# Tail products of a two-layer encoder taken 512 columns wide with tokens as rows, and two more weight groups split by adding transfers

## The chip, the cores and the metric

The kernel runs on one core of one Trainium2 chip. The metric is device time in microseconds (us) of one execution, as the median of several runs. The kernel before takes 1712.34 us (three runs, 1711.75 to 1714.05).

The core's engines are named as the profile names them: PE is the matrix engine (PEld are its weight loads), DVE the vector engine, ACT the scalar engine, POOL the general-purpose engine, SP the engine that only issues transfers here. Each engine takes its instructions in the order in which they are written. A matmul multiplies a stationary operand (loaded by PEld, 128 x 128 here) with a moving operand that streams past it, and adds into a PSUM bank of 128 partitions x 512 float32.

## The reference

256 tokens of width 1024 pass two layers. Each layer normalises, projects to 18688 columns, runs three token mixers, and merges them by token-wise gates:

```python
for l in range(DEPTH):
    h = rmsnorm(x, norm_g[l])
    proj = h @ w_in[l]                     # 1024 x 18688
    (a_q, a_ff, a_fb, a_i, a_g, b_q, b_k, b_v, b_g, c_s, c_g, merge) = split(proj)
    y_a = hgrn2_mixer(a_q, a_ff, a_fb, a_i, ...) * silu(a_g)      # 256 x 1024
    y_b = retention_mixer(b_q, b_k, b_v, ...) * silu(b_g)         # 256 x 2048
    y_c = rwkv7_mixer(c_s, ...) * silu(c_g)                       # 256 x 1024
    gates = sigmoid(merge.reshape(b, t, 3, 1024))
    mixed = (gates[:, :, 0] * (y_a @ w_branch_a[l])
             + gates[:, :, 1] * (y_b @ w_branch_b[l])
             + gates[:, :, 2] * (y_c @ w_branch_c[l]))
    x = x + mixed @ w_out[l]
return rmsnorm(x, final_norm_g)
```

## The kernel before

**Precision.** Every product with a weight matrix is made of three float32r matmuls: a value v is split into hi (v rounded to float32r) and lo (v - hi), and a*b is taken as hi*hi + lo*hi + hi*lo. Float32r runs the PE faster than plain float32; the mixers' own small products are plain float32, and each of those stands as two matmul records in the trace.

**Weights.** Weights are laid out ahead of time in blocks of 1024 x 256, each as two halves of 128 partitions x 1024 numbers (512 KB). A half passes through rings of buffers: `in` (3), `hi` (5), `lo` (4). There are two ways to split it. The usual one: SP transfers the raw half into an `in` buffer, ACT copies it with rounding into `hi` (a CAST), DVE subtracts `hi` from the raw half into `lo`. The other one, for the block names in `CCE` (mixer A's five groups): POOL issues a transfer into `hi` that rounds, ACT writes its negative into `lo`, and POOL issues a second transfer of the same half that adds onto `lo`. This needs no `in` buffer and no DVE work, but two POOL-issued transfers.

**A layer** has two parts. In the first, mixer C runs in eight steps (head pairs p): `c_prep` and `c_solve` run two steps ahead of `c_scan`; between them stand the four `a_pair` steps (p = -1 to 2), then the four `b_pair` steps (p = 3 to 6). A `b_pair` projects query and key (blocks `bq`, `bk`), and for each of two heads value and gate (`bv`, `bg`): six blocks, twelve halves. `c_solve` needs a small POOL MEMSET of the diagonal of `c_M` before its DVE chain, and `c_prep` one of `c_ux`. In the second part, `tail`, the mixers' outputs (reloaded and split by `load_y`) are merged. For mixer m and column block b of 256 (four of them), the tail makes the gate's projection (`mg`), its sigmoid on ACT and DVE, the branch product (one weight block, two for B), multiplies by the gate and adds to the accumulator. Before the change the stationary operand in these is the weight (128 output features) and the moving one the activations of all 256 tokens (`feat_mm`): outputs have features as partitions, so the accumulators can be the stationary operand of the last product (`tok_mm`, `wo`), whose output has tokens as partitions. Every float32r matmul of the kernel streams 256 columns.

**Order.** Nothing is issued as written. All operations are recorded (`note`), with what each waits for (`parts` finds overlaps by pieces of 16 columns x 32 partitions); `cost` estimates each, and `order` places them by a list schedule, whose result is each engine's fixed program order. So all instructions carry the line of the one loop that issues them: L453 before, L460 after. `cost` and `order` hold the planner's figures for transfers and matmuls; a change in them moves instructions on every engine.

**Names in the trace.** `pj` and `c` (two PSUM banks each) hold the weight products, `n`, `s`, `ab` the mixers' small ones. `w_in`, `w_hi`, `w_lo` are the weight rings. In the tail, which reuses the mixers' buffers under names ending in `_t`, `ab_ex_t`/`ab_e_t` are mixer A's split output, `c_Z_t` B's, `c_rkvg_t`/`c_tu_t` C's, `ab_vg_t` the gates, `ab_kq_t`/`ab_c_t` the accumulators, `c_wa_t`/`c_qm_t` the split merged value (`m_hi`, `m_lo`), `c_bd_t` the residual x.

Of the kernel before, what the change touches and what calls it, by code (L numbers as in the profile page):

```python
# [19 lines left out]
D = 1024  # L20
# [4 lines left out]
TOK = ("ai", "bv", "wo")  # L25
# [3 lines left out]
CCE = ('aff', 'afb', 'aq', 'ai', 'ag')  # L29
# [34 lines left out]
def _blocks():  # L64
# [8 lines left out]
    for p in range(4):  # L73
        r.append((("bq", p), "w_in", 0, [(5120 + 256 * p, 256)]))
        r.append((("bk", p), "w_in", 0, [(6144 + 256 * p, 256)]))
        for h in (2 * p, 2 * p + 1):
            r.append((("bv", h), "w_in", 0, [(7168 + 256 * h, 256)]))
            r.append((("bg", h), "w_in", 0, [(9216 + 256 * h, 256)]))
    for m in range(3):
        for b in range(4):  # L80
            c = 256 * b
            r.append((("mg", m, b), "w_in", 0, [(15616 + 1024 * m + c, 256)]))
            for n, w, r0 in ((("wa", "w_branch_a", 0),), (("wb0", "w_branch_b", 0), ("wb1", "w_branch_b", 1024)),
                             (("wc", "w_branch_c", 0),))[m]:
                r.append(((n, b), w, r0, [(c, 256)]))
    for b in range(4):
        r.append((("wo", b), "w_out", 0, [(256 * b, 256)]))
# [3 lines left out]
for _i, _b in enumerate(_blocks()):  # L91
    BK[_b[0]] = _i
assert len(BK) == NBLK
# [28 lines left out]
class Plan:  # L122
# [3 lines left out]
    def __init__(self, ctx, tc, some):  # L126
# [4 lines left out]
        self.homes, self.base, self.top, self.place, self.turn, self.psum, self.ndram, self.cache = {}, {}, 0, {}, {}, {}, 0, {}  # L131
        self.last, self.readers, self.bank, self.fill = {}, {}, {}, {}
        self.width, self.tenant, self.before = dict(HOMES), {}, {}
        self.width.update({f"w_{k}{i}": 1024 for k, m in RW.items() for i in range(m)})
        for n, k in BANKS:
            for i in range(k):
                t = self.pp.tile([128, 512], F32, name=f"{n}{i}")[:, :]
                self.psum[n, i] = t
                self.base[t.tensor.name] = (None, f"{n}{i}")
# [3 lines left out]
    def home(self, n, era, dt):  # L143
        old = self.tenant.get(n)
        if old is None or self.tiles[old][1] != era:
            k, w = len(self.tiles), self.width[n]
            if old is not None:
                top, size = self.tiles[old][3], 4 * (w // 16 + 2)
                self.before[k] = {p for g in range(top, top + size) for p in [self.last.get(g, -1)] + self.readers.get(g, [])} - {-1}
            self.tiles.append((n, era, dt, self.top, bass.AP(tensor=self.some.tensor, offset=k << 20, ap=[[w, 128], [1, w]]), w))  # L150
            self.top += 4 * (w // 16 + 2)
# [3 lines left out]
    def real(self, ap):  # L155
# [3 lines left out]
        if k not in self.made:  # L159
            n, era, dt, _, _, w = self.tiles[k]  # L160
# [47 lines left out]
    def dram(self):  # L208
        plan = self

        class Dram:
            def tile(self, shape, dt, name, tag=None):
                plan.ndram += 1
                t = plan.dp.tile(shape, dt, name=f"{name}_{plan.ndram}")[:]
                plan.base[t.tensor.name] = (plan.top, 0)
                plan.top += int(np.prod(shape)) // 32 + 1
# [10 lines left out]
    def parts(self, ap):  # L227

        off = int(ap.offset)
        if ap.tensor.name == self.some.tensor.name:  # L230
            if off < 1 << 20:
                return ()
            _, _, _, base, _, w = self.tiles[off >> 20]
            off &= (1 << 20) - 1
        else:
            b = self.base.get(ap.tensor.name)
            if b is None:
                return ()
            base, w = b
            if base is None:  # L240
                return w
        dims = tuple((int(s), int(c)) for s, c in ap.ap)
        key = (base, off, dims)
        r = self.cache.get(key)
        if r is None:
            if w:
                p, c = divmod(off, w)
                ix = np.array([c])
                for s, n in dims[1:]:
                    if s:  # L250
                        ix = (ix[:, None] + s * np.arange(n)).ravel()
                ix = np.unique(ix // 16)
                r = [base + 4 * int(i) + q for q in range(p // 32, (p + dims[0][1] - 1) // 32 + 1) for i in ix]
            else:
                ix = np.array([off])
                for s, n in dims:
                    if s:
                        ix = np.unique((ix[:, None] + s * np.arange(n)).ravel())
                r = [base + int(i) for i in np.unique(ix // 32)]
            self.cache[key] = r  # L260
        return r
# [12 lines left out]
    def note(self, eng, op, args, kw):  # L274
# [4 lines left out]
        pred, true, rd, wr, fresh = set(), set(), [], [], False  # L279
        for a, w in aps:  # L280
            p = self.parts(a)
            if isinstance(p, str):
                if p in self.bank:
                    pred.add(self.bank[p])
                self.bank[p] = n
            else:
                (wr if w else rd).extend(p)
                if w and (op == "copy_predicated" or "accum_op" in kw):
                    rd.extend(p)
        last, readers = self.last, self.readers  # L290
        for g in rd:
            if g in last:
                true.add(last[g])
        for g in wr:
            if g in last:
                pred.add(last[g])
                pred.update(readers.get(g, ()))
            else:
                fresh = True
        if fresh and out.tensor.name == self.some.tensor.name:  # L300
            pred |= self.before.get(int(out.offset) >> 20, set())
        for g in rd:
            readers.setdefault(g, []).append(n)
        for g in wr:
            last[g] = n
            readers[g] = []
# [6 lines left out]
    def cost(self, eng, op, out, ins, args, kw):  # L313
# [3 lines left out]
        def psum(a):  # L317
            return self.base.get(a.tensor.name, (0,))[0] is None

        both = False  # L320
        if op == "dma_start":
# [4 lines left out]
            return (380. if eng == "sync" else 1000.), b / (330. if run >= 512 else 330. * max(run, 64) / 512), both  # L326
        if eng == "tensor":
            n, m = size(out), size(ins[-1])
# [43 lines left out]
    def order(self):  # L372
# [26 lines left out]
        use, slow = {}, {0: False}  # L399

# [6 lines left out]
        for _ in range(N):  # L407
# [13 lines left out]
            if e == "tensor":  # L421
# [3 lines left out]
                while x < at + hold:  # L425
# [3 lines left out]
                    x = y  # L429
            start[n], now[e] = at, at + hold  # L430
            moves = o[1] == "dma_start"
            if moves:
                dma = max(at + (700. if e == "sync" else 1500.), dma) + o[6]
                end = dma + 1100. + HOP
            for s in succ[n]:
# [21 lines left out]
def trunk(ctx: ExitStack, tc, x, wb, pp, lora, cst, gtab, ng, out):  # L457
# [68 lines left out]

    def load_w(l, key):

        W = []
        for h in range(2):  # L530
            src = wb[2 * (l * NBLK + BK[key]) + h]
            hi, lo = plan.weight("hi"), plan.weight("lo")
            if key[0] in CCE or key in CCE:

                G.dma_start(hi, src)
                S.activation(lo, hi.bitcast(F32), AF.Copy, scale=-1.0)
                G.dma_start(lo, src, accum_op=ALU.add)
            else:
                raw = plan.weight("in")
                SY.dma_start(raw, src)  # L540
                S.copy(hi, raw)
                V.tensor_sub(lo, raw, hi.bitcast(F32))
            W.append((hi, lo))
        return W

# [564 lines left out]
    def tail(l, ya, yb, yc, x_src, early, pool):  # L1110
        acc = [early.tile([128, 2, T], F32, name=f"t_acc{b}") for b in range(4)]
        Y, xs = [], None
        for m in range(3):
            br = ((("wa", 0),), (("wb0", 1), ("wb1", 2)), (("wc", 3),))[m]
            for b in range(4):
                o = proj(l, ("mg", m, b))
                g = early.tile([128, 2, T], F32, tag="t_g", bufs=TG, name="t_g")
                S.activation(g, o, AF.Exp, scale=-1.0)
                sigmoid_of_exp(g)
# [176 lines left out]
```

## Time and profile before

| | us |
|---|---|
| median of three runs | 1712.34 |
| the profiled execution | 1706.83 |
| its span, first to last instruction | 1705.0 |
| PE busy | 1627.3 (95%) |
| DVE busy | 1265.2 (74%) |
| ACT busy | 1131.8 (66%) |
| POOL busy | 132.4 (8%) |

The mean granted PE clock is 0.987. In the span, the first layer's mixer part lasts from about 0 to 650 us, its tail to about 850; the second layer's mixer part to about 1500, its tail to 1697; the last 8 us are the closing norm and its output. A PE instruction's recorded duration includes its way through the array, so it is longer than the distance at which matmuls follow each other, and "busy" is the union of these.

### The profile page before, as it was taken

How to read it: one execution, taken by the hardware profiler on the slowest of the kernel's cores; microseconds unless marked ns; L12 is line 12 of the kernel's file. 1: busy time of each engine (PE TensorE's matmuls, PEld its weight loads, DVE VectorE, ACT ScalarE, POOL GpSimd, SP SyncE). 2: the span in 40 equal slices, each digit the busy share in tenths (PEclk: the TensorE clock that was granted, in tenths of full speed). 3: DMA queues.
4: the chain of work that ended last, by engine and by line, in shares of the span. 5: the costliest groups of instructions: out<-in, count | busy, mean ns of one | idle time of the engine just before them, and what ended most of it. 6: DMA issues, size and time to landing. Idle time of an engine off the chain costs nothing.

```text
span 1705.0 us, 33613 instructions
## 1 busy us (share of the span) xinstructions
PE 1627.3 (95%) x12960; PEld 1594.7 (94%) x12960; DVE 1265.2 (74%) x2613; ACT 1131.8 (66%) x2196; POOL 132.4 (8%) x216
## 2 busy tenths in 40 slices
PE   6989999999999999999998899999999999999997
PEld 6878999999999999999898799998899999999997
DVE  5598889897777986555557888899967878865554
ACT  5877778775756757545559587878657567665553
POOL 1211121100000000000021111220000000000000
PEclk9999999999999999999989899999999999999999
DMA  7968788645455456565568767885454554565653
GB/s 247 233 159 187 173 179 206 142 146 169 120 159 143 124 164 223 177 198 185 189 201 190 174 146 207 198 189 111 134 181 117 171 137 136 169 209 178 199 183 103
DMA packets 139392, 292.24 MB, mean 171 GB/s; under 512 B 63584, under 2 KB 68064, under 8 KB 138976
## 3 DMA queue, kind: packets, MB, share of 16 engines
q1 hardware_dynamic: 116192, 206.20, 39.9%
q0 software_dynamic: 23040, 83.90, 22.0%
q8 instruction: 102, 1.67, 0.4%
q14 instruction: 58, 0.48, 0.1%
HBM read 271.17 MB, written 14.68 MB: 168 GB/s over the span
## 4 chain that ended last, share of the span: by engine, by line
PE 70%; DVE 8%; DMA 8%; issue 7%; ACT 6%; POOL 1%; SPq 1%; DVEq 0%; POOLq 0%; ACTq 0%
PE pj L453 38%; PE c L453 16%; PE n L453 9%; PE ab L453 5%; DMA w_in<-in_wb_dram 2%; PE s L453 2%; DMA w_hi<-in_wb_dram 2%; DVE c_tq L453 2%; DMA ab_ex<-ab_ex 1%; DVE w_lo L453 1%; DVE ab_e L453 1%; ACT c_ux L453 1%; ACT w_hi L453 1%; SPq L453 1%; DVE ab_p L453 1%
## 5 line engine op out<-in xcount | busy, mean ns | idle before, releaser
L453 PE MATMUL pj<-h_hi,w_hi 128*128 128x256 f32 x1952 | 562.3, 297 | 10.3 <-ACT ab_e L453 3.5
L453 PE MATMUL pj<-h_hi,w_lo 128*128 128x256 f32 x1952 | 558.3, 295 | 1.7 <-DMA w_lo<-in_wb_dram 1.0
L453 PE MATMUL pj<-h_lo,w_hi 128*128 128x256 f32 x1952 | 553.5, 292 | 0.1
L453 DVE TENSOR_TENSOR w_lo<-w_in,w_hi 128x1024 fp32r<-128x1024 f32 x292 | 354.3, 1220 | 178.3 <-PE pj L453 47.9
L453 ACT CAST w_hi<-w_in 128x1024 fp32r<-128x1024 f32 x292 | 305.2, 1049 | 206.9 <-PE pj L453 70.0
L453 PEld LDWEIGHTS pj<-h_hi,w_hi 128*128 128x128 f32 x1952 | 369.9, 193 | 14.9 <-ACT ab_e L453 3.7
L453 PEld LDWEIGHTS pj<-h_hi,w_lo 128*128 128x128 f32 x1952 | 369.0, 193 | 4.1 <-DMA w_lo<-in_wb_dram 1.4
L453 PEld LDWEIGHTS pj<-h_lo,w_hi 128*128 128x128 f32 x1952 | 369.8, 193 | 2.2 <-DVE h_lo L453 0.6
L453 PE MATMUL pj<-w_lo,h_hi 128*128 128x256 f32 x384 | 111.6, 291 | 2.7 <-DMA w_lo<-in_wb_dram 2.7
L453 PE MATMUL pj<-w_hi,h_hi 128*128 128x256 f32 x384 | 112.5, 293 | 1.4 <-ACT ab_ex L453 1.4
L453 PE MATMUL c<-c_Z,c_bd 128*128 128x192 f32 (+1 forms) x512 | 106.3, 309 | 7.6 <-ACT c_bd L453 4.6
L453 PE MATMUL pj<-w_hi,h_lo 128*128 128x256 f32 x384 | 110.5, 288 | 0.0
L453 PE MATMUL c<-c_Z_t,w_hi 128*128 128x256 f32 x512 | 95.7, 284 | 0.0
L453 ACT COPY c_y<-n 128x128 f32<-128x128 f32 (+1 forms) x160 | 61.8, 392 | 45.8 <-PE n L453 43.7
L453 PEld LDWEIGHTS c<-c_Z,c_bd 128*128 128x128 f32 x512 | 80.6, 196 | 10.2 <-ACT c_bd L453 6.6
L453 ACT ACTIVATE w_lo<-w_hi 128x1024 fp32r<-128x1024 f32 x80 | 84.4, 1056 | 7.7 <-DMA w_hi<-in_wb_dram 5.6
L453 POOL DMA_DIRECT2D w_lo<-in_wb_dram x80 | 71.2, 891 | 175.8 <-ACT w_lo L453 76.2
L453 PE MATMUL n<-c_y,c_wa 128*128 128x128 f32 x512 | 81.1, 279 | 2.5 <-ACT c_y L453 1.5
L453 DVE TENSOR_TENSOR c_tq<-c_W,c_M 128x16 f32<-128x16 f32 (+6 forms) x112 | 81.9, 732 | 1.4
L453 PE MATMUL ab<-ab_e 128*128 128x128 f32 x448 | 73.7, 286 | 8.3 <-DVE ab_p L453 2.5
L453 PEld LDWEIGHTS c<-c_Z_t,w_hi 128*128 128x128 f32 x512 | 79.0, 190 | 0.2
L453 PEld LDWEIGHTS pj<-w_lo,h_hi 128*128 128x128 f32 x384 | 73.3, 191 | 3.8 <-DMA w_lo<-in_wb_dram 3.4
(195 smaller groups left out, 3604.9 us busy)
## 6 DMA issues: line engine op xcount, KB each, us to landing
w_in<-in_wb_dram SPq DMA_DIRECT2D x292, 512.0 KB, 3.8
w_hi<-in_wb_dram POOLq DMA_DIRECT2D x80, 512.0 KB, 5.4
w_lo<-in_wb_dram POOLq DMA_DIRECT2D x80, 512.0 KB, 7.1
c_M<-s SPq DMA_DIRECT2D x64, 128.0 KB, 5.0
c_ux<-in_lora_dram SPq DMA_DIRECT2D x16, 256.0 KB, 2.8
ab_e<-in_gtab_dram SPq DMA_DIRECT2D x16, 256.0 KB, 2.7
ab_ex<-ab_ex SPq DMA_DIRECT2D x16, 256.0 KB, 5.5
yb<-ab_e SPq DMA_DIRECT2D x16, 256.0 KB, 4.0
```

Source lines behind the costliest of these rows:

```text
L453: getattr(getattr(self.tc.nc, eng), op)(*map(self.real, args), **{k: self.real(v) for k, v in kw.items()})
```

## The change

**The merge by token.** The blocks of the tail (`mg`, `wa`, `wb0`, `wb1`, `wc`, `wo`) become 512 columns wide, each as four halves of 128 partitions x (2 x 512). The new `wide_mm` makes the activations (128 tokens) the stationary operand and 512 weight columns the moving one; two PSUM banks, one for each half of the tokens, are filled together. Gates, accumulators and branch products therefore have tokens as partitions. Since the last product needs the merged value with features as partitions, each accumulator is transposed on the PE (four transposes of 128 x 128 into an `n` bank) before ACT and DVE split it. `wo` now fills two `pj` banks (first 512 columns) and two `c` banks (last 512).

**Exact records.** `parts` and `note` find overlaps by exact bit masks.

**The planner's figures.** POOL-issued transfers get a longer latency (3300 instead of 2600), shorter issue times, and at most eight outstanding per queue (`SLOTS`); the size that sets a small float32 matmul's estimate is that of the stationary operand.

**B's query and key blocks** join `CCE`: 16 halves a layer, 32 in all.

```diff
-TOK = ("ai", "bv", "wo")
+TOK = ("ai", "bv")
+WIDE = ("mg", "wa", "wb0", "wb1", "wc", "wo")
-CCE = ('aff', 'afb', 'aq', 'ai', 'ag')
+CCE = ("bq","bk",'aff', 'afb', 'aq', 'ai', 'ag')
...
-            return (380. if eng == "sync" else 1000.), b / (...), both
+            return (380. if eng == "sync" else 870. if "accum_op" in kw else 550.), b / (...), both
-            n, m = size(out), size(ins[-1])
+            n, m = size(out), size(ins[0])
-                return (1800. if a[0] == "sync" else 2600.) + a[6] + HOP
+                return (1800. if a[0] == "sync" else 3300.) + a[6] + HOP
+        SLOTS, land = 8, {e: [] for e in ENGINES}
+            if moves and len(land[e]) >= SLOTS:
+                at = max(at, land[e][-SLOTS] + HOP)
...
+    def wide_mm(l, key, o, h, first=True, last=True):
+        hhi, hlo = h
+        for k in range(KT):
+            if k % 2 == 0:
+                whi, wlo = (w.rearrange("p (k c) -> p k c", c=512) for w in load_half(l, key, k // 2))
+            for t in range(2):
+                r = slice(128 * t, 128 * t + 128)
+                for i, (a, b) in enumerate(((hhi, whi), (hlo, whi), (hhi, wlo))):
+                    PE.matmul(o[t], a[:, k, r], b[:, k % 2], start=(first and k == 0 and i == 0),
+                              stop=(last and k == KT - 1 and i == 2))
...
-            for b in range(4):
-                o = proj(l, ("mg", m, b))
+            for b in range(2):
+                o = [ps.tile([128, 512], F32, tag="pj") for t in range(2)]
+                wide_mm(l, ("mg", m, b), o, (h_hi, h_lo))
...
-                o = [ps.tile([128, 256], F32, tag="c", name="t_o") for f in range(2)]
+                o = [ps.tile([128, 512], F32, tag="c") for t in range(2)]
                 for i, (key, y) in enumerate(br):
-                    W = load_w(l, (key, b))
-                    for f in range(2):
-                        feat_mm(o[f], W, f, Y[y], first=(i == 0), last=(i == len(br) - 1))
+                    wide_mm(l, (key, b), o, Y[y], first=(i == 0), last=(i == len(br) - 1))
...
+                for t in range(2):
+                    s = acc[2 * t + b]
+                    V.tensor_mul(gs[t] if m else s, o[t], gs[t])
+                    if m:
+                        V.tensor_add(s, s, gs[t])
+                    if m == 2:
+                        x = ps.tile([128, 4, 128], F32, tag="n", name="t_t")
+                        for k in range(4):
+                            PE.transpose(x[:, k], s[:, 128 * k:128 * k + 128], ident)
+                        r = m_hi[:, 4 * b:4 * b + 4, 128 * t:128 * t + 128]
+                        S.copy(r, x)
+                        V.tensor_sub(m_lo[:, 4 * b:4 * b + 4, 128 * t:128 * t + 128], x, r.bitcast(F32))
...
-        for b in range(4):
-            W = load_w(l, ("wo", b))
-            o = ps.tile([128, 2, 256], F32, tag="pj")
+        for b in range(2):
+            o = [ps.tile([128, 512], F32, tag="c" if b else "pj") for t in range(2)]
+            wide_mm(l, ("wo", b), o, (m_hi, m_lo))
...
-                V.tensor_add(xs[:, t, r], xs[:, t, r], o[:, t])
+                V.tensor_add(xs[:, t, r], xs[:, t, r], o[t])
                 S.activation(sq, xs[:, t, r], AF.Square, accum_out=s4[:, t, b:b + 1])
```

Two places show how the order moves. The first is PE where the second layer's last branch product ends and the last product (`wo`) begins; before:

```order
L453 MATMUL c_67<-c_rkvg_t,w_hi_182 128x256
L453 MATMUL c_67<-c_tu_t,w_hi_182 128x256
L453 MATMUL c_67<-c_rkvg_t,w_lo_209 128x256
L453 MATMUL pj_64<-w_hi_200,c_wa_t 128x256
L453 MATMUL pj_64<-w_hi_200,c_qm_t 128x256
L453 MATMUL pj_64<-w_lo_146,c_wa_t 128x256
```

and after, from the eleventh matmul of the last product on:

```order
L460 MATMUL pj_65<-w_hi_242,c_qm_t 128x512
L460 MATMUL n_68<-cst,ab_kq_t 128x128
L460 MATMUL pj_64<-w_lo_159,c_wa_t 128x512
L460 MATMUL n_68<-cst,ab_kq_t 128x128
L460 MATMUL pj_65<-w_lo_159,c_wa_t 128x512
L460 MATMUL n_68<-cst,ab_kq_t 128x128
L460 MATMUL n_69<-cst,ab_c_t 128x128
L460 MATMUL n_68<-cst,ab_kq_t 128x128
L460 MATMUL n_69<-cst,ab_c_t 128x128 x3
L460 MATMUL pj_64<-w_hi_149,c_wa_t 128x512
```

Matmuls of 512 columns in two banks by turns stand in the place of those of 256, and the eight transposes of the last two accumulators stand inside the last product.

The second is POOL in the first layer's mixer B part; before it holds only the small MEMSETs:

```order
L453 MEMSET c_ux 128x8
L453 MEMSET c_M 128x32
L453 MEMSET c_ux 128x8
L453 MEMSET c_M 128x32
L453 MEMSET c_ux 128x8
L453 MEMSET c_M 128x32
```

and after they stand between the new transfers:

```order
L460 DMA w_lo_184<-in_wb_dram 128x1024
L460 MEMSET c_M 128x32
L460 DMA w_hi_217<-in_wb_dram 128x1024
L460 DMA w_hi_242<-in_wb_dram 128x1024
L460 DMA w_lo_193<-in_wb_dram 128x1024
L460 DMA w_hi_149<-in_wb_dram 128x1024
L460 MEMSET c_ux 128x8
L460 DMA w_hi_154<-in_wb_dram 128x1024
L460 DMA w_lo_236<-in_wb_dram 128x1024
L460 DMA w_lo_159<-in_wb_dram 128x1024
L460 DMA w_lo_184<-in_wb_dram 128x1024
L460 MEMSET c_M 128x32
```

Each MEMSET of `c_M` and `c_ux` now waits in POOL's queue behind transfers that wait for free weight buffers or for ACT.

More of the change, by code (lines that the diff above doesn't have):

```diff
@@ L147, in home @@
             if old is not None:
[L148 to L151, printed above, removed]
+                self.before[k] = {p for x in self.live.get(old, ()) for _, p in x}
+            self.tiles.append((n, era, dt, w, bass.AP(tensor=self.some.tensor, offset=k << 20, ap=[[w, 128], [1, w]])))
             self.tenant[n] = k
@@ L230, in parts @@
         if ap.tensor.name == self.some.tensor.name:
[L231 to L233 removed]
+            where = off >> 20
+            if not where:
+                return None, 0
+            w = self.tiles[where][3]
             off &= (1 << 20) - 1
         else:
[L236 to L241, printed above, removed]
+            where = ap.tensor.name
+            w = self.base.get(where, -1)
+            if w is None or w < 0:
+                return (where if w is None else None), 0
         dims = tuple((int(s), int(c)) for s, c in ap.ap)
[L243 removed]
+        key = (w, off, dims)
         r = self.cache.get(key)
@@ L278, in note @@
         out, ins = aps[0][0], [a for a, w in aps if not w]
-        pred, true, rd, wr, fresh = set(), set(), [], [], False
+        pred, true, acc = set(), set(), []
         for a, w in aps:
[L281 to L306, printed above, removed]
+            where, m = self.parts(a)
+            if where is None:
+                continue
+            if not m:
+                if where in self.bank:
+                    pred.add(self.bank[where])
+                self.bank[where] = n
+                continue
+            acc.append((where, m, w))
+            wrote, read = self.live.setdefault(where, ([], []))
+            if not w or op == "copy_predicated" or "accum_op" in kw:
+                true.update(p for x, p in wrote if x & m)
+            if w:
+                pred.update(p for x, p in wrote if x & m)
+                pred.update(p for x, p in read if x & m)
+                if m & ~self.covered.get(where, 0):
+                    pred |= self.before.get(where, set())
+        for where, m, w in acc:
+            wrote, read = self.live[where]
+            if w:
+                wrote[:] = [(x & ~m, p) for x, p in wrote if x & ~m]
+                read[:] = [(x & ~m, p) for x, p in read if x & ~m]
+                self.covered[where] = self.covered.get(where, 0) | m
+        for where, m, w in acc:
+            self.live[where][0 if w else 1].append((m, n))
         true = {p for p in true if self.ops[p][0] != eng or eng != "tensor"}
@@ L524, in trunk, with load_half @@
     V.tensor_scalar(omlb, lb, -1.0, 1.0, op0=ALU.mult, op1=ALU.add)
-    def load_w(l, key):
[L529 to L544, printed above, removed]
+    def load_half(l, key, h):
+        src = wb[2 * (l * NBLK + BK[key]) + h]
+        hi, lo = plan.weight("hi"), plan.weight("lo")
+        if key[0] in CCE:
+            G.dma_start(hi, src)
+            S.activation(lo, hi.bitcast(F32), AF.Copy, scale=-1.0)
+            G.dma_start(lo, src, accum_op=ALU.add)
+        else:
+            raw = plan.weight("in")
+            SY.dma_start(raw, src)
+            S.copy(hi, raw)
+            V.tensor_sub(lo, raw, hi.bitcast(F32))
+        return hi, lo
+    def load_w(l, key):
+        return [load_half(l, key, h) for h in range(2)]
+    def wide_mm(l, key, o, h, first=True, last=True):
[8 more added lines that the diff above has]
+                              stop=(last and k == KT - 1 and i == 2))
     def feat_mm(o, W, f, h, first=True, last=True):
@@ L1110, in tail @@
     def tail(l, ya, yb, yc, x_src, early, pool):
-        acc = [early.tile([128, 2, T], F32, name=f"t_acc{b}") for b in range(4)]
+        acc = [early.tile([128, 512], F32, name=f"t_acc{i}") for i in range(4)]
         Y, xs = [], None
@@ L1140, in tail @@
+        s4 = pool.tile([128, 2, 2], F32, name="t_s4")
         ss = pool.tile([128, 2], F32, name="t_ss")
```

106 lines of the change are left out of this document (54 added, 52 removed).

## The prediction

> **What bounds the kernel now.** I read the page first: its busy times and the chain that ended last.
>
> ```profile
> span 1705.0 us, 33613 instructions
> PE 1627.3 (95%) x12960; PEld 1594.7 (94%) x12960; DVE 1265.2 (74%) x2613; ACT 1131.8 (66%) x2196; POOL 132.4 (8%) x216
> PE 70%; DVE 8%; DMA 8%; issue 7%; ACT 6%; POOL 1%; SPq 1%; DVEq 0%; POOLq 0%; ACTq 0%
> ```
>
> PE is busy for 95% of the span and is 70% of the chain: only fewer or shorter matmuls, or fewer PE stalls, shorten this kernel. Next the view of busy time by stretches, cut at the stages: the columns are the stretch, its length, then busy us of PE, PEld, DVE, ACT, POOL, and the granted clock.
>
> ```profile
> 0.00:160.00 160.00, 131.84 (x979) 125.66 (x980) 114.51 (x273) 111.55 (x214) 33.82 (x56) 0.98 0.82 212
> 160.00:340.00 180.00, 178.48 (x1456) 175.70 (x1456) 152.82 (x371) 141.41 (x303) 31.47 (x47) 1.00 0.77 174
> 340.00:650.00 310.00, 302.43 (x2399) 295.36 (x2399) 250.88 (x516) 203.33 (x426) 0.98 (x7) 1.00 0.51 148
> 650.00:850.00 200.00, 197.62 (x1652) 196.93 (x1650) 116.24 (x147) 112.79 (x160) 2.16 (x3) 1.00 0.59 192
> 850.00:1000.00 150.00, 133.07 (x966) 127.50 (x967) 106.34 (x254) 104.21 (x210) 28.84 (x47) 0.92 0.71 183
> 1000.00:1160.00 160.00, 160.00 (x1320) 158.49 (x1320) 140.45 (x352) 124.61 (x265) 32.40 (x48) 1.00 0.81 191
> 1160.00:1500.00 340.00, 328.92 (x2570) 320.87 (x2569) 271.90 (x562) 226.66 (x466) 2.77 (x10) 0.98 0.50 144
> 1500.00:1697.00 197.00, 194.95 (x1631) 194.18 (x1629) 109.43 (x140) 105.84 (x151) 0.00 (x0) 1.00 0.56 177
> ```
>
> The two tails (650 to 850, 1500 to 1697) are PE alone: 99% busy, DVE and ACT near 57%. Mixer B's stretches (340 to 650, 1160 to 1500) leave PE idle for 7.6 and 11.1 us, with 2% of the clock gone in the second (about 6.8 us): 25.5 us in all. Mixer A's later stretches (160 to 340, 1000 to 1160), where POOL issues A's weights, leave only 1.5 us. So two questions decide: what a 512-column matmul costs, and what POOL's transfers do to B.
>
> **The tail's matmuls.** Each layer's tail has 12 gate blocks, 16 branch blocks and 4 last blocks of 48 matmuls: 1536 of 256 columns, now 768 of 512. Both layers: 1536 pairs become 1536 single ones. The price of the old is the chain's row of the last product (start, length, count); for the new, no row exists, so I read durations (min/median/max ns) of both kinds of matmul by tile.
>
> ```profile
> 1673.04 23.05 PE pj L453 x192
> L453 PE MATMUL pj<-w_hi,c_wa_t x128: 283/283/283, 824.7 to 1695.6; 128*128 128x256 f32 x128
> L453 PE MATMUL n<-c_y,c_wa x512: 270/275/421, 152.3 to 1523.3; 128*128 128x128 f32 x171
> L453 PE MATMUL n<-c_y,cst x64: 377/378/433, 175.1 to 1566.4; 128*128 128x256 f32 x64
> 155.91 1.55 PE pj L453 x13
> 157.46 1.56 PE n L453 x14
> ```
>
> Old: 23.05 / 192 = 0.120 us each, 0.240 a pair. Plain float32 goes from 275 to 378 ns when its columns double from 128 to 256: 103 ns for 128 columns. A float32r matmul of 256 columns (283) lasts about as long as a plain one of 128 (275), so I take a float32r column at half a plain one's price: 256 more columns cost 103 ns, and a 512-column matmul follows the last at 120 + 103 = 223 ns. Of the 120, 17 ns are then a fixed part, paid half as often. Ends: 206 (2 x 103, no fixed part is left) and 240 (all of the 120 goes by columns). Taken: 223, from the rows that differ in columns alone. Saved: 1536 x 17 ns = **26.1 us** (52 to 0).
>
> By the Trainium skill, "TensorE: Matmul & The Clock Gate", section "Back-to-back issue gap", matmuls follow at columns / 2.4 + 2.5 ns, which is 215.8 ns at 512 and would save 1536 x 24.2 ns = 37.2 us, an estimate. The same rule gives 109.2 ns at 256, and the row here shows 120, so this trace disagrees with it, and the sum goes by the rows.
>
> **What the tail adds.** Sixteen transposes a layer, 32 in all. A 128-column record in the `n` banks costs 1.56 / 14 = 0.111 us, and a transpose is one record: **+3.6 us** on PE. Eight of them a layer wait for DVE behind the last branch product. There DVE has four operations of 512 columns to do for the two halves of the tokens. The rows for this, and for the tail's end:
>
> ```profile
> L453 DVE TENSOR_TENSOR ab_kq_t<-ab_kq_t,ab_vg_t x12: 685/692/692, 730.2 to 1665.3; 128x512 f32<-128x512 f32 x12
> L453 ACT ACTIVATE ab_vg_t<-ab_vg_t x48: 616/632/637, 655.7 to 1670.4; 128x512 f32<-128x512 f32 x48
> 1696.11 0.75 DVE L453 TENSOR_TENSOR c_bd_t<-c_bd_t,pj 128x256 f32<-128x256 f32 x2 [2.00 <-PE pj L453]
> 1696.63 0.42 ACT L453 ACTIVATE c_y_t<-c_bd_t 128x256 f32<-128x256 f32 x1 [1.85 <-DVE c_bd_t L453]
> 1697.57 0.16 DVE L453 TENSOR_REDUCE c_W_t<-c_W_t 128x2 f32<-128x8 f32 x1 [0.70 <-ACT c_y_t L453]
> ```
>
> 4 x 0.69 = 2.8 us; in the order the first transpose stands behind eleven matmuls (2.5 us) and the last three behind thirteen (2.9 us): covered by matmuls whose operands were ready earlier, within 0.5 us, taken as 0. Behind them stand eleven more matmuls that need only the first column block, 2.5 us, while ACT copies (0.6) and DVE subtracts (0.7).
>
> At a layer's end both halves of the tokens now finish together. Before, one add of 256 columns (0.42, from 1696.11) and a square (0.42) followed the last matmul; now two adds of 512 (0.69 each) and a square of 512 (0.63): 2.0 against 0.84, **+1.2 us**, twice: +2.4. Nothing covers it: the next norm waits.
>
> PSUM: a gate takes both `pj` banks, which drain while the branch product (48 x 0.223 = 10.7 us) fills both `c` banks; two ACT reads of 0.6 us are done long before.
>
> **B's query and key.** The groups of the page for the splitting, its issue rows (us to landing), then from 340 to 650 alone the subtraction's row by tile and PE's two longest waits:
>
> ```profile
> L453 DVE TENSOR_TENSOR w_lo<-w_in,w_hi 128x1024 fp32r<-128x1024 f32 x292 | 354.3, 1220 | 178.3 <-PE pj L453 47.9
> L453 ACT CAST w_hi<-w_in 128x1024 fp32r<-128x1024 f32 x292 | 305.2, 1049 | 206.9 <-PE pj L453 70.0
> L453 ACT ACTIVATE w_lo<-w_hi 128x1024 fp32r<-128x1024 f32 x80 | 84.4, 1056 | 7.7 <-DMA w_hi<-in_wb_dram 5.6
> w_in<-in_wb_dram SPq DMA_DIRECT2D x292, 512.0 KB, 3.8
> w_hi<-in_wb_dram POOLq DMA_DIRECT2D x80, 512.0 KB, 5.4
> w_lo<-in_wb_dram POOLq DMA_DIRECT2D x80, 512.0 KB, 7.1
> L453 DVE TENSOR_TENSOR w_lo<-w_in,w_hi x64: 1190/1220/1227, 349.0 to 649.7; 128x1024 fp32r<-128x1024 f32 x64
> PEld n L453 <- ACT c_y L453: 2.2, 3, 1.2
> PEld pj L453 <- DVE ab_vg L453: 2.2, 2, 1.2
> ```
>
> In the tail a half now lasts 12 x 223 = 2.7 us on PE (2.9 before) and needs 1.05 us of ACT and 1.22 of DVE: weights stay covered there. In B, 32 halves lose a DVE subtraction of 1.22 us: 39 us of DVE, 19.5 of the 250.9 it works from 340 to 650 (81% to 75%). ACT keeps its pass (1049 against 1056 ns). A half's way gets longer: 3.8 + 1.05 + 1.22 = 6.1 us before, 5.4 + 1.06 + 7.1 = 13.6 now. With the 2.9 us of its matmuls a `hi` buffer is then held 16.5 us, so five buffers carry one half per 3.3 us; That stretch used 64 halves in 310 us, one per 4.8. It fits. PE's waits in B are many and short, on ACT and DVE results that came late by a microsecond or two; less DVE work shortens a part of them. The gain lies between 0 and the 25.5 us above; most rows name ACT, which is not relieved, so I take a quarter: **-6 us**. The loss side is the second rival below.
>
> The planner's other figures move everything else. The starts of A (0 to 160, 850 to 1000) lose far more than B, but with DVE or the first weights late; I take 0 and allow 10 us either way.
>
> **Sum** against the profiled execution: 1706.8 - 26.1 + 3.6 + 2.4 - 6 = 1680.7. The median of the runs shown, 1712.3, lies 5.5 above that execution; on its scale the sum is 1686.2.
>
> **Rivals.**
>
> *The fixed part falls away.* One weight load stands by each matmul (x12960 both), and there are now half as many in the tail; if the 17 ns are the load showing and 512 columns hide it, matmuls follow at 206 ns: 52 saved in place of 26, 1660. For it: PEld is 94% busy. Against it: the plain `n` matmuls, also one load each, follow at 111 ns with 103 for their columns. The skill's rule above lies on this side, at 1675.
>
> *POOL's queue holds up mixer C in B.* The MEMSETs of `c_M` and `c_ux`, on which C's DVE chain waits, now stand behind transfers that wait for buffers or for ACT. Such a place is in the second layer's start (stretches as above, then POOL's instructions):
>
> ```profile
> 940.00:960.00 20.00, 15.64 (x94) 14.54 (x93) 19.95 (x52) 10.45 (x26) 1.43 (x2) 0.83 0.38 92
> 960.00:980.00 20.00, 16.48 (x108) 15.97 (x107) 13.25 (x33) 11.69 (x26) 4.83 (x7) 0.83 1.04 256
> 1020.00:1040.00 20.00, 20.00 (x170) 20.00 (x169) 19.90 (x48) 15.29 (x37) 2.50 (x4) 1.00 0.67 163
> 948.61 0.89 POOL L453 DMA_DIRECT2D w_lo<-in_wb_dram  x1 [6.93 <-ACT c_Z L453]
> 961.49 0.55 POOL L453 DMA_DIRECT2D w_hi<-in_wb_dram  x1 [11.99 <-DVE ab_p L453]
> ```
>
> From 940 to 980 PE did 202 records where a full stretch does 340: 138 x 0.12 = 16.6 us lost, half of it to the lower clock that follows an idle PE. Two such stalls in the run eat the 20.1 us of the tail's gain; one in each of B's first two pairs of each layer makes four, 66 us less the 20.1: 1759; two give 1725 with B's gain gone. Against it: A's later stretches have this queue and lose 1.5 us.
>
> *All of the 120 ns goes by columns.* Then 26.1 is 0, and 1712.3 + 3.6 + 2.4 - 6 = 1712: no change. For it: float32r matmuls follow at 120 ns wherever they stand in a row, which one width cannot split. Against it: plain matmuls have a fixed part of some 8 ns.
>
> *The order does not do what it says*, PE waiting in the tail for weights or transposes: 2 us a block in 32 blocks would undo the gain, 1750. Against it: DVE and ACT near 57%.
>
> **How the numbers follow.** Forecast 0.51, fixed part gone 0.15, by columns 0.12, POOL's queue 0.17, waits in the tail 0.05. Time: **1686 us**. The likeliest's own range, with B from 0 to 15 us and the planner's 10, is 1672 to 1700; to leave out no more than 2 in 10 I go to 1664 (half of the fixed-part rival and most of B's gain) and 1717 (beyond the by-columns case and a mild queue). A change under 0.2% (3.4 us) cannot be told from none. Faster: 0.49 of the forecast, 0.15, 0.04 of by-columns, 0.02 of POOL's: 0.70. Same: 0.02, 0.05, 0.03, 0.02: 0.12. Slower: the rest, 0.18.
>
> **What would show it.** In the changed profile: 512-column matmuls in the last product following at 0.22 us (0.206 or 0.240 for the rivals), each with a duration near 386 ns; tails shorter by 9 to 14 us each; the last matmul to the closing norm 1.2 us longer; DVE's `w_lo` group at 260 and POOL's two at 112 each; B's stretches with less PE idle than 18.7 us. I am wrong if B's stretches show POOL waits that end in PE idling with the clock below 1.00, or if the 512-column matmuls cost two of 256.

## The result and the profile after

The changed kernel takes 1666.9 us (median of four runs, 1663.41 to 1675.49) against 1712.05 before: ratio 0.9743, 95% interval 0.9705 to 0.9781. The profiled execution has a span of 1661.6 us against 1705.0, so 43.4 us are to be found in the two traces.

The head of the page after, and its rows for the chain, the splitting by DVE and the issues of weight transfers:

```profile
span 1661.6 us, 30708 instructions
PE 1602.2 (96%) x11456; PEld 1510.7 (91%) x11456; DVE 1227.9 (74%) x2549; ACT 1128.7 (68%) x2180; POOL 179.5 (11%) x280
PE 82%; DVE 6%; DMA 5%; ACT 5%; issue 2%; SPq 0%; DVEq 0%; POOL 0%; ACTq 0%; POOLq 0%
L460 DVE TENSOR_TENSOR w_lo<-w_in,w_hi 128x1024 fp32r<-128x1024 f32 x260 | 316.8, 1222 | 153.4 <-PE pj L460 62.8
w_in<-in_wb_dram SPq DMA_DIRECT2D x260, 512.0 KB, 4.3
w_hi<-in_wb_dram POOLq DMA_DIRECT2D x112, 512.0 KB, 5.2
w_lo<-in_wb_dram POOLq DMA_DIRECT2D x112, 512.0 KB, 6.7
```

PE's records fall from 12960 to 11456 (1536 matmuls less, 32 transposes more), and PE is now 82% of the chain instead of 70%. PE busy falls by 25.1 us; the other 18.3 us of the span were time in which PE stood idle. The matmuls of the tail: three stretches of the chain of waits (start, us, count), and behind them two rows by tile (min, median and max duration in ns):

```profile
693.04 10.88 PE pj L460 x48
703.92 10.88 PE c L460 x48
813.52 5.52 PE pj L460 x24
```

```profile
L460 PE MATMUL c<-w_hi,c_qm_t x32: 387/389/397, 819.3 to 1651.7; 128*128 128x512 f32 x32
L460 PE MATMUL n<-cst,ab_kq_t x24: 270/270/272, 798.3 to 1632.6; 128*128 128x128 f32 x24
```

A 512-column matmul follows the last at 10.88 / 48 = 0.2267 us, 13.3 ns less than two of 256 (in the last product 5.52 / 24 = 0.230). Then the end, by the timeline:

```profile
1652.38 1.28 DVE L460 TENSOR_TENSOR c_bd_t<-c_bd_t,c 128x512 f32<-128x512 f32 x2 [5.87 <-PE c L460]
1653.16 0.63 ACT L460 ACTIVATE c_y_t<-c_bd_t 128x512 f32<-128x512 f32 x1 [7.01 <-DVE c_bd_t L460]
1654.53 0.16 DVE L460 TENSOR_REDUCE c_W_t<-c_W_t 128x2 f32<-128x4 f32 x1 [0.86 <-ACT c_y_t L460]
```

From the first add to the closing sum it takes 2.15 us, against 1.46 before (1696.11 to 1697.57).

To see where PE lost time, I cut both traces at the same points of the work: mixer C's eight scans of a layer (the first matmul into `s` of each), and the last matmul of the layer's last product. In each stretch "lost" is its length less PE's records times the distance at which such records follow when nothing stalls: 120 ns (float32r, 256 columns), 226.6 (512), 215.5, 162.5, 110 and 80 (plain float32 of 256, 192, 128 and 64), as the traces show them from start to start. Worked out from all PE records of a trace, in us:

| stretch | lost before | lost after |
|---|---|---|
| first layer: start to first scan | 39.3 | 34.7 |
| first to third scan | 3.9 | 8.0 |
| third to fifth scan (mixer A hands over to B) | 9.2 | 6.6 |
| fifth to eighth scan (B) | 8.7 | 4.0 |
| eighth scan to the layer's last matmul | 0.4 | 1.8 |
| second layer: start to first scan | 33.2 | 24.8 |
| first to third scan | 2.3 | 5.7 |
| third to fifth scan | 16.3 | 4.6 |
| fifth to eighth scan | 9.8 | 4.5 |
| eighth scan to the last matmul | 0.4 | 2.5 |
| the end | 9.1 | 9.2 |
| sum | 132.7 | 106.4 |

PE's work by the same distances falls by 17.1 us (1572.3 to 1555.2), the losses by 26.3: together 43.4. Most of the losses' part comes from the hand-over and B (24.3 us) and from the second layer's start (8.4); the two layers' starts together give 13.0. The view of busy time by stretches for the second layer, third to fifth scan and fifth to eighth, before:

```profile
1147.00:1311.00 164.00, 156.94 (x1214) 152.84 (x1214) 130.14 (x278) 114.33 (x239) 5.16 (x10) 0.97 0.50 138
1311.00:1557.00 246.00, 240.85 (x1933) 236.34 (x1932) 186.79 (x352) 156.21 (x296) 0.55 (x4) 1.00 0.56 168
```

and after:

```profile
1127.00:1279.00 152.00, 150.90 (x1213) 147.89 (x1212) 122.65 (x268) 115.93 (x239) 17.13 (x25) 1.00 0.68 171
1279.00:1534.00 255.00, 254.04 (x1797) 238.82 (x1796) 184.69 (x349) 165.91 (x310) 12.12 (x21) 1.00 0.67 193
```

The hand-over does as many records (1213 against 1214) in 152 us in place of 164, with PE idle for 1.1 us instead of 7.1 and the full clock. (The second stretch after holds some of the tail's gates, so its length is not to be compared.)

### The profile page after: what moved, and what is told of

The parts are those of the page before. It is cut to its first block, busy times and chain, and to the rows that moved or that the text cites. A ratio compares the mean times of both kernels' runs of the same rounds, so it can differ in the third digit from the quotient of the medians.

```text
span 1661.6 us, 30708 instructions
## 1 busy us (share of the span) xinstructions
PE 1602.2 (96%) x11456; PEld 1510.7 (91%) x11456; DVE 1227.9 (74%) x2549; ACT 1128.7 (68%) x2180; POOL 179.5 (11%) x280
## 4 chain that ended last, share of the span: by engine, by line
PE 82%; DVE 6%; DMA 5%; ACT 5%; issue 2%; SPq 0%; DVEq 0%; POOL 0%; ACTq 0%; POOLq 0%
PE pj L460 43%; PE c L460 17%; PE n L460 12%; PE ab L460 7%; PE s L460 2%; DMA w_in<-in_wb_dram 1%; DMA w_lo<-in_wb_dram 1%; DVE c_tq L460 1%; DVE ab_e L460 1%; DVE w_lo L460 1%; ACT c_ux L460 1%; ACT w_hi L460 1%; DMA w_hi<-in_wb_dram 1%; ACT w_lo L460 1%; DVE c_Z L460 1%
## 5 line engine op out<-in xcount | busy, mean ns | idle before, releaser
L460 PE MATMUL pj<-h_hi,w_hi 128*128 128x256 f32 x1568 | 460.0, 300 | 5.4 <-DVE ab_kq L460 2.2
L460 PE MATMUL pj<-h_hi,w_lo 128*128 128x256 f32 x1568 | 457.2, 299 | 2.5 <-DMA w_lo<-in_wb_dram 2.5
L460 PE MATMUL pj<-h_lo,w_hi 128*128 128x256 f32 x1568 | 457.0, 296 | 1.1 <-DVE h_lo L460 1.1
L460 PEld LDWEIGHTS pj<-h_hi,w_hi 128*128 128x128 f32 x1568 | 297.9, 193 | 9.3 <-DVE ab_kq L460 3.0
L460 PEld LDWEIGHTS pj<-h_hi,w_lo 128*128 128x128 f32 x1568 | 297.4, 192 | 5.5 <-DMA w_lo<-in_wb_dram 3.6
L460 PE MATMUL pj<-w_lo,h_hi 128*128 128x256 f32 (+1 forms) x576 | 176.6, 331 | 1.1 <-DMA w_lo<-in_wb_dram 1.1
L460 PE MATMUL pj<-w_hi,h_hi 128*128 128x256 f32 (+1 forms) x576 | 176.2, 330 | 0.0
L460 PE MATMUL pj<-w_hi,h_lo 128*128 128x256 f32 (+1 forms) x576 | 174.5, 328 | 0.0
L460 PEld LDWEIGHTS pj<-w_hi,h_hi 128*128 128x128 f32 x576 | 110.6, 193 | 7.2
L460 PEld LDWEIGHTS pj<-w_hi,h_lo 128*128 128x128 f32 x576 | 110.5, 192 | 7.1
```

The lines of the kernel that those rows point to most:

```text
L460: getattr(getattr(self.tc.nc, eng), op)(*map(self.real, args), **{k: self.real(v) for k, v in kw.items()})
```

## The experiments

The change has four parts: exact records (E), the merge by token (M), the planner's new figures (P), and B's query and key by POOL (C). Seven of the kernels below combine the last three on top of exact records (the changed kernel is the eighth); none of the three was run without E. The others move the order alone or B's transfers. All times are medians of four or five runs. The kernels below were timed in three sessions, in which the kernel before took 1713.0, 1713.1 and 1713.8 us; "us less" is against these.

**Exact records alone.**

```diff
 # the kernel before, with parts() and note() of the change
-                ix = np.unique(ix // 16)
+            flag[ix] = 1
+            r = m = int.from_bytes(np.packbits(flag, bitorder="little").tobytes(), "little")
```

> The kernel before with the exact records alone: no merge by token, the old planner's figures, B's query and key split as before. Theory A (the gain beyond the tail's 17 us of PE work comes from B's query and key going by POOL's transfers): within 5 us of before, 1707 to 1717. Theory B (it comes from the planner's figures for transfers): the same, 1707 to 1717. Theory C (any new order gives or takes about 10 us, and this change drew a good one): anywhere from 1700 to 1725.

Measured 1684.4 us, ratio 0.9839 (0.9792 to 0.9885): 28 us less, with not one operation changed. I had thought of this part as bookkeeping. Theories A and B did not foresee it; C allows any order some 10 us, and this is more. By the measure of the table above this trace loses 111.2 us, 21.5 less than the kernel before, and 14.0 of these lie in the two layers' starts (34.4 and 24.1 us lost there).

**Exact records and the planner's figures.**

```diff
 # as above, and
-            return (380. if eng == "sync" else 1000.), ...
+            return (380. if eng == "sync" else 870. if "accum_op" in kw else 550.), ...
-            n, m = size(out), size(ins[-1])
+            n, m = size(out), size(ins[0])
-                return (1800. if a[0] == "sync" else 2600.) + a[6] + HOP
+                return (1800. if a[0] == "sync" else 3300.) + a[6] + HOP
+            if moves and len(land[e]) >= SLOTS:
+                at = max(at, land[e][-SLOTS] + HOP)
```

> The kernel before with the exact records and the planner's new figures (POOL latencies, eight outstanding transfers, the size that sets a small matmul's estimate); no merge, B split as before. Theory A: 1705 to 1717, the figures alone give nothing, and B's stretches of PE (340 to 650, 1160 to 1500) keep their 18 us of idle. Theory B: 1684 to 1692, with most of the gain in the second layer between 850 and 1250. Theory C: anywhere from 1700 to 1725.

Measured 1696.8 us, ratio 0.9903 (0.9873 to 0.9934): 12 us more than exact records alone, and in none of the three ranges. Theory B falls: the figures do not bring the gain.

**Exact records and the merge.**

```diff
 # the changed kernel, with the planner's old figures, and
-CCE = ("bq","bk",'aff', 'afb', 'aq', 'ai', 'ag')
+CCE = ('aff', 'afb', 'aq', 'ai', 'ag')
```

> The kernel before with the exact records and the merge by token; the old planner's figures, B split as before. From the 226.7 ns of a 512-column matmul in the changed kernel: 1536 x 13.3 = 20.4 us less PE work, 3.5 for 32 transposes, 2.4 for the two ends: 14.5 us less than the same without the merge, so 1698 if all else stays. Theory A and B: 1695 to 1702. Theory C: 1685 to 1710.

Measured 1685.7 us, ratio 0.984 (0.9805 to 0.9876): no better than exact records alone (14.5 us less would have been 1670) and in Theory C's range alone, though its PE work is 17.1 us less. Its trace lost that much elsewhere: by the measure of the table above 129.2 us against 111.2, of it 6.8 from the fifth to the eighth scans of both layers, 5.4 in the tails behind the eighth, and 2.9 at the hand-overs.

**The changed kernel without B's transfers.**

```diff
-CCE = ("bq","bk",'aff', 'afb', 'aq', 'ai', 'ag')
+CCE = ('aff', 'afb', 'aq', 'ai', 'ag')
```

> The changed kernel, with B's query and key blocks split by ACT and DVE as before. Theory A: the 28 us beyond the merge are gone, 1692 to 1700, with B's stretches idle on PE as before (18 us). Theory B: 1667 to 1675, within 5 us of the changed kernel. Theory C: 1680 to 1700 without a place that holds most of the difference.

Measured 1681.9 us, ratio 0.983 (0.9789 to 0.9871): 15 us over the changed kernel. Theory B's range is missed, Theory A's too, on the low side: B's transfers are worth 15 us here and the other parts 31 together. Theory C's range holds the time, but its condition fails, for the difference has a place: of the 18.4 us that this trace loses more than the changed kernel's, 11.5 lie at the hand-overs and 7.0 in B behind them.

**Another order of the kernel before.** Since exact records change the order alone, the next question is what any change of order is worth.

```diff
-        return [60. * n - d for n, d in enumerate(depth)]
+        return [62. * n - d for n, d in enumerate(depth)]
```

> The kernel before with one number of the planner's rank changed (62 ns instead of 60 for each operation's place in the recorded order), which moves instructions on all engines and changes no work. If exact records really remove 28 us (theory D), this stays at 1705 to 1720. If a new order by itself is worth some 15 us either way (theory C), it lies anywhere from 1685 to 1725, and a result under 1700 or above 1720 speaks for C.

Measured 1693.0 us, ratio 0.9892 (0.9868 to 0.9916): 20 us less, from one number that says nothing of the hardware. Theory C holds to this extent: the kernel before stood on a poor order beside this one, and single differences of 10 to 20 us between kernels whose orders differ cannot be put down to what was meant to be changed.

**Exact records and B's transfers.**

```diff
 # exact records alone, and
-CCE = ('aff', 'afb', 'aq', 'ai', 'ag')
+CCE = ("bq","bk",'aff', 'afb', 'aq', 'ai', 'ag')
```

> Exact records and B's query and key by POOL's transfers; no merge, the old planner's figures. Beside the exact records alone (1684). Theory A (B's transfers give 15 us of their own, as between the changed kernel and the same without them): 1665 to 1673, with PE's loss between 1150 and 1500 down from 17 to 8 us. Theory C: 1675 to 1695.

Measured 1670.6 us, ratio 0.9756 (0.973 to 0.9781), as Theory A said. Busy time by stretches of the first layer, third to fifth scan and fifth to eighth, with exact records alone:

```profile
301.00:462.00 161.00, 155.39 (x1218) 151.66 (x1217) 127.57 (x269) 115.31 (x238) 5.52 (x10) 0.98 0.50 141
462.00:706.00 244.00, 240.42 (x1935) 236.44 (x1935) 185.90 (x352) 157.61 (x296) 0.55 (x4) 1.00 0.56 170
```

and with B's transfers as well:

```profile
301.00:454.00 153.00, 151.55 (x1226) 149.20 (x1225) 120.25 (x262) 114.47 (x243) 16.49 (x26) 1.00 0.68 176
454.00:696.00 242.00, 239.75 (x1931) 235.85 (x1930) 176.41 (x343) 157.01 (x296) 11.95 (x20) 1.00 0.66 188
```

Eight of the ten microseconds of this layer are gained at the hand-over, where the last of mixer A's DVE work and B's first subtractions fall together. DVE does 7 instructions less there (269 to 262), as many as its subtractions for weights fall (26 to 19), PE's idle time falls from 5.6 to 1.4 us, and the clock's dip goes. Finer stretches of the same place, with exact records alone:

```profile
320.00:340.00 20.00, 19.83 (x160) 19.24 (x158) 19.96 (x48) 19.51 (x42) 0.11 (x1) 1.00 0.34 75
340.00:360.00 20.00, 18.18 (x131) 17.84 (x132) 18.48 (x42) 13.20 (x33) 0.16 (x1) 0.91 0.51 151
360.00:380.00 20.00, 19.29 (x155) 18.36 (x154) 19.95 (x59) 14.78 (x31) 0.00 (x0) 1.00 0.44 135
```

and with B's transfers:

```profile
320.00:340.00 20.00, 20.00 (x161) 19.69 (x160) 19.65 (x45) 19.27 (x38) 3.35 (x7) 1.00 0.72 199
340.00:360.00 20.00, 20.00 (x166) 19.67 (x165) 19.93 (x52) 18.79 (x49) 2.60 (x3) 1.00 0.89 204
360.00:380.00 20.00, 20.00 (x171) 19.84 (x170) 16.95 (x49) 11.94 (x29) 0.16 (x1) 1.00 0.38 120
```

DVE is nearly full here in both (58.4 and 56.5 of 60 us), but PE gets 498 records done instead of 446. Between 320 and 380 us there are seven subtractions for weights in place of nine, and between 340 and 360 one in place of four. The chain of work that ended last, from 340 to 360 us, tells the difference; in the kernel before, with exact records alone, and with B's transfers as well:

```profile
by line: DMA w_in<-in_wb_dram 30.3%; DVE w_lo L453 16.8%; PE c L453 16.6%; DVE c_Z L453 7.0%; DVE c_ux L453 6.3%; DVE ab_p L453 5.2%; PE n L453 5.1%; DVE ab_e L453 5.0%; PE ab L453 4.5%; DVE ab_vg L453 3.0%; DVE c_y L453 1.7%; issue 0.8%
by line: DVE ab_e L457 28.3%; PE c L457 20.3%; DVE w_lo L457 17.0%; DVE ab_p L457 9.9%; PE ab L457 8.8%; issue 6.1%; DVE c_Z L457 4.2%; PE n L457 3.4%; DVE c_rkvg L457 2.0%; PE pj L457 1.8%
by line: PE ab L457 26.7%; PE n L457 26.7%; PE pj L457 23.8%; PE c L457 23.1%
```

Without B's transfers the subtractions `w_lo`, between the mixers' own DVE work, hold 17% of the chain in both kernels, and before the raw transfers `w_in` another 30%; with them the chain is PE alone.

**The changed kernel with the planner's old figures.**

```diff
-                return (1800. if a[0] == "sync" else 3300.) + a[6] + HOP
+                return (1800. if a[0] == "sync" else 2600.) + a[6] + HOP
 # and the other figures as before
```

> The changed kernel with the planner's old figures: exact records, merge, and B's query and key by POOL. Theory A: the figures matter little, 1663 to 1673. Theory B' (the figures matter only where POOL issues more transfers): 1678 to 1690, with PE idle behind POOL's queue in B. Theory C: 1665 to 1690.

Measured 1662.2 us (1660.17 to 1666.79), ratio 0.9711 (0.9687 to 0.9736), just under Theory A's range: the fastest kernel of this case, 4.7 us under the changed one, whose interval it overlaps. The new figures are not needed where POOL issues more, either.

**The changed kernel without the merge.**

```diff
-TOK = ("ai", "bv")
-WIDE = ("mg", "wa", "wb0", "wb1", "wc", "wo")
+TOK = ("ai", "bv", "wo")
+WIDE = ()
 # and tail() and the blocks of 256 columns of the kernel before
```

> The changed kernel without the merge by token: exact records, new figures, B's query and key by POOL. If the merge gives its 14.5 us: 1678 to 1684. If the merge gives nothing, as between the exact records alone (1684) and those with the merge (1686): 1663 to 1670.

Measured 1686.1 us (1682.65 to 1693.74), ratio 0.9851 (0.9819 to 0.9883): 19 us over the changed kernel, a little past the 14.5 that the merge's own rows give. So the eight combinations are (us):

| | without C | with C | C brings |
|---|---|---|---|
| E | 1684.4 | 1670.6 | -13.8 |
| E, M | 1685.7 | 1662.2 | -23.5 |
| E, P | 1696.8 | 1686.1 | -10.7 |
| E, P, M | 1681.9 | 1666.9 | -15.0 |

B's transfers gain in all four pairs, 15.8 on the mean. The merge gains 10.3 on the mean (+1.3, -8.4, -14.9, -19.2), the figures lose 7.2 (+12.4, +15.5, -3.8, +4.7). Each part's four differences spread by 5 to 9 us (standard deviation); new orders and the runs' own spread (3 to 12 us within one kernel) can both make that. The kernels without C ran in one session and those with it in others. All eight have the same rank in the planner; the runs with another rank follow below.

**The first pair only.**

```diff
 # exact records alone, and
-CCE = ('aff', 'afb', 'aq', 'ai', 'ag')
+CCE = (('bq', 0), ('bk', 0), 'aff', 'afb', 'aq', 'ai', 'ag')
-        if key[0] in CCE:
+        if key[0] in CCE or key in CCE:
```

> Exact records, old figures, no merge, and of mixer B's query and key blocks only those of the first pair by POOL (4 halves a layer in place of 16). Between exact records alone (1684.4) and with all four pairs (1670.6). If the gain is at the hand-over from mixer A to B, where DVE is full: 1671 to 1677, with PE's loss between mixer C's third and fifth scan down from 13.0 and 9.2 us to about 4 and 5, and from the fifth to the eighth as without (7.6 and 8.1). If it is spread over B: 1680 to 1684. If orders by chance decide: 1670 to 1695, with the losses moved elsewhere.

Measured 1679.5 us, ratio 0.9817 (0.9791 to 0.9842): 4.9 us of the 13.8, between the two ranges. The same two stretches of its trace:

```profile
300.00:456.00 156.00, 152.22 (x1217) 149.47 (x1216) 123.77 (x265) 113.64 (x241) 10.71 (x18) 0.99 0.60 158
456.00:701.00 245.00, 241.03 (x1938) 236.89 (x1938) 186.42 (x352) 157.80 (x296) 0.54 (x4) 1.00 0.56 169
```

Four halves bring the hand-over from 161 to 156 us and leave the rest of B as it was (245 against 244). By the measure of losses the hand-overs fall from 13.0 and 9.2 to 8.2 and 5.7; the second layer's start, which the edit does not touch, lost 3.9 us more in this order, and so the whole shows less. The place shows in the trace, and that it holds the larger part of C's gain is so in the traces; this kernel's time does not decide, since it lies within the range of chance orders too.

**Exact records with the other rank.**

```diff
-        return [60. * n - d for n, d in enumerate(depth)]
+        return [62. * n - d for n, d in enumerate(depth)]
```

> Exact records alone, with 62 in the planner's rank in place of 60. If exact records are worth something of their own beyond a lucky order: 1680 to 1692, below the kernel before with 62 (1693). If the 28 us were a lucky order: 1690 to 1710.

Measured 1682.5 us, ratio 0.9822 (0.9787 to 0.9857). Of the 28 us of exact records at rank 60, 10.6 are left at rank 62 (1693.0 to 1682.5). Exact records gain in both pairs; how much of it is theirs in general two pairs don't fix.

**The changed kernel with the other rank.** The same edit on the changed kernel:

> The changed kernel with 62 in the planner's rank. If its time stands on its work and transfers: 1662 to 1674. If it is a lucky order: 1675 to 1695.

Measured 1678.6 us, ratio 0.9809 (0.9782 to 0.9836): 11.7 us more. So the changed kernel stands on a good order beside this one. At rank 62 the whole change is worth 14.5 us (1693.0 to 1678.6), at rank 60 it is worth 45. Of the 14.5, 10.6 come with exact records, and the merge, the figures and B's transfers together bring only 3.9 (1682.5 to 1678.6), where they bring 17.5 at rank 60. The table above holds for its rank; no run takes B's transfers alone at the other.

The measure of losses over all traces tells what stays when the order changes. In the two layers' starts the twelve kernels with exact records lose 58 to 65 us, the two without lose 72.5 and 67.2. At the two hand-overs the six kernels with all of B's query and key by POOL lose 9.3 to 13.9 us; of the seven with none of it six lose 21.9 to 25.5, and one, exact records at rank 62, loses 13.8. There an order did nearly what the transfers do elsewhere.

**B's gates by POOL too.** From the fastest kernel, an attempt to gain more in the same way:

```diff
-CCE = ("bq","bk",'aff', 'afb', 'aq', 'ai', 'ag')
+CCE = ("bq","bk","bg",'aff', 'afb', 'aq', 'ai', 'ag')
```

> The fastest so far (exact records, merge, B's query and key by POOL, old figures: 1662.2) with B's gate blocks by POOL too: 32 more halves, 39 us less of DVE work, 64 more POOL transfers. If DVE is still what PE's stalls in B wait for: 1652 to 1660. If POOL's queue becomes the wait: 1665 to 1685, with PE idle in B behind POOL.

Measured 1695.8 us, ratio 0.9912 (0.9882 to 0.9943): 34 us worse, beyond both ranges. The first layer from the fifth to the eighth scan in the fastest kernel:

```profile
452.00:708.00 256.00, 253.94 (x1794) 238.76 (x1792) 185.07 (x348) 166.21 (x309) 12.27 (x20) 1.00 0.68 191
```

and with the gates:

```profile
460.00:723.00 263.00, 254.00 (x1759) 236.20 (x1759) 172.07 (x339) 167.05 (x313) 26.76 (x41) 0.99 0.75 202
```

POOL's longest waits from 340 to 650 in the kernel with the gates (us in total, times, longest):

```profile
POOL w_hi L458 <- PE pj L458: 85.8, 18, 13.0
POOL w_lo L458 <- ACT w_lo L458: 65.3, 17, 9.5
```

and the same waits in the fastest kernel:

```profile
POOL w_hi L458 <- PE pj L458: 126.7, 10, 50.1
POOL w_lo L458 <- ACT w_lo L458: 11.7, 7, 4.4
```

In the stretch from the fifth to the eighth scan PE is idle for 9.0 us in place of 2.1, while DVE does less (172 against 185). By the measure of losses 23.3 of the 32.4 us between the two traces lie between these scans of the two layers. The chain of the same stretch, in the fastest kernel and with the gates:

```profile
by line: PE pj L458 52.9%; PE c L458 18.3%; PE n L458 14.5%; PE ab L458 7.2%; PE s L458 3.2%; DMA w_in<-in_wb_dram 2.3%; ACT w_hi L458 0.8%; DVE w_lo L458 0.5%; ACT c_y L458 0.2%; issue 0.1%; ACTq L458 0.0%
by line: PE pj L458 40.6%; PE c L458 12.7%; PE n L458 11.7%; PE ab L458 4.6%; DMA w_in<-in_wb_dram 3.8%; DMA w_lo<-in_wb_dram 3.5%; ACT c_ux L458 3.2%; PE s L458 2.7%; ACT w_lo L458 2.4%; issue 1.7%; DMA ab_p_t<-yb 1.5%; ACT ab_vg L458 1.3%
```

Already in the fastest kernel DVE held only 0.5% of this chain, so there was little left to gain from relieving it. With the gates, POOL's transfers onto `lo` waited 65 us for ACT's negative, against 11.7, and these transfers (3.5%) and the negatives (2.4%) now stand in the chain, which they did not before; POOL's MEMSETs do not stand in it at all. That POOL's way of splitting is the new wait fits this. No run here separates it from a poor order, which by the runs above can cost 10 to 20 us.

## Why the prediction was right or wrong

The forecast was faster, 1686 us in a range of 1664 to 1717; 1666.9 lies near its lower end and below the likeliest's own range (1672 to 1700). The direction stood, and the merge and B's transfers gain as said; the sizes were off, and part of the agreement is luck.

- **The 512-column matmul**: 223 ns was taken, 226.7 measured. The fixed part is 13.3 ns, not 17; the saving 1536 x 13.3 = 20.4 us, not 26.1. The estimate took 103 ns for 256 more columns from the recorded durations of plain float32; the distance of float32r matmuls grows by 106.7. The rival that it falls away (206) and the one by columns (240) are both out; so is the rule of the Trainium skill's page "TensorE: Matmul & The Clock Gate", section "Back-to-back issue gap" (215.8 by the formula, which that section gives for a single matmul; 11 ns under the rows).
- **Transposes**: 32 at about 0.11 us on PE, as said, and no wait for DVE stands before them in the trace after.
- **The ends**: +1.2 us each was taken; it is +0.69. The side before was read too short: behind the last matmul stood two adds and two squares of 256 columns (the second square starts at 1697.04), not one of each, and to the closing sum they took 1.46 us, not 0.84. After, it is two and two as well, 2.15 us where I had 2.0: the first square starts after the first add.
- **B's query and key**: -6 us was taken, with 0 to 25.5 as ends; the four pairs give -10.7 to -23.5, mean -15.8. My reason for a quarter (most rows name ACT) was too simple: in the kernel with exact records alone DVE was busy for 58.4 of 60 us at the hand-over. That a result which ACT delivers late had waited for DVE before is argued, not traced.
- **Luck in the sum**: the merge was taken at -20.1 us (26.1 less 3.6 and 2.4) and brings -10.3 on the mean of its four pairs; B's transfers were taken at -6 and bring -15.8. Each miss is 9.8 us, and the two cancel by chance.
- **"Fits in the buffers, POOL's queue holds nothing up"**: right for B's query and key, with whose transfers the kernel was faster in all four pairs. With B's gates as well the kernel takes 34 us more, though in the first layer's stretch not by the rival's mechanism, the MEMSETs.
- **The planner's figures, 0 with 10 us either way**: this term held the order of every instruction and was the largest unknown. The layers' starts, put at 0 here, lose 13.0 us less in the trace after. The figures lose 7 us on the mean; the exact records, which I passed over, gain 10.6 and 28 in two pairs; one number in the rank moves the kernel before by 20 us and the changed one by 12. The term should have been some 20 us either way. The time came out 19 us under the forecast mainly for this: as the misses of the merge and of B's transfers cancel, what is left is roughly the 28 us of exact records at this rank, less the 7 of the figures. At rank 62 the whole change brings 14.5 us, less than the 26 of the forecast. Beside rank 62, the kernel before had drawn a poor order and the changed one a good one.
- **The tail**: "shorter by 9 to 14 us each" was too much. Its PE work falls by 8.5 us a layer, of which 1.4 and 2.1 us are lost again behind the eighth scan.

What stays open: how much of the exact records' gain is theirs, and what makes an order good. In all traces here the exact records shorten the layers' starts; they free the planner of waits between neighbours in a 16-column piece, but no run here shows which of these count.

## What to carry to other kernels

Where a planner fixes the order of 30 thousand instructions, any edit redraws the order, and the redraw here was worth 10 to 20 us: time both kernels under a second order before a gain of one per cent is put down to the edit. An engine at 60 to 80% on the whole can be full in the one stretch where two stages overlap; here, at one rank of the planner, moving a little of its work away gained as much as a shorter inner loop in the tail, and moving twice as much lost it all again.

## What was not expected of the hardware

Float32r matmuls of 256 and 512 columns follow at 120 and 226.7 ns: 106.7 ns for 256 columns and 13.3 ns for each matmul, the same in branch products and gates, and up to 230 ns in the last product. A 512 KB transfer issued by POOL lands after 5.2 us, one that adds after 6.7, and one by SP after 4.3 (medians of the changed kernel): the longer way was no loss here: PE's waits from 340 to 650 us in the changed kernel name none of these transfers.
